# A decoder layer on one core: the moving operands of the split products stored with tokens reversed and read with step minus one

## The chip, the cores and the metric

The kernel runs on one core of one Trainium2 chip, in one launch. The metric is the device time of the launch in microseconds. Work on the host (laying out weights, transposing the input and the output) is not part of it.

## The reference, cut to what matters

One layer on 512 tokens of width 1024, all in float32. Three blocks are added to the residual stream in turn:

```python
x = x + 0.5 * swiglu(rms_norm(x, g_ffn1), w_ffn1_gate, w_ffn1_up, w_ffn1_down)
proj = rms_norm(x, g_mix) @ w_in          # q, k, v, u, mq
...                                       # window attention, conv module, memory attention
x = x + concatenate([y_attn, y_conv, y_mem], axis=-1) @ w_out
x = x + 0.5 * swiglu(rms_norm(x, g_ffn2), w_ffn2_gate, w_ffn2_up, w_ffn2_down)

def swiglu(x, w_gate, w_up, w_down):
    return (silu(x @ w_gate) * (x @ w_up)) @ w_down
```

The hidden width of each SwiGLU is 2816, 22 tiles of 128. The middle block projects to queries, keys, values, a gated convolution input and memory queries. It does attention in a window of 128 tokens with a sink per head, a causal convolution of 31 taps with a layer norm, and attention into 256 memory tokens, and projects the three results back. Almost all of the arithmetic is in the matrix products with weights.

## The kernel before, in words

**Layout.** Features lie on the 128 partitions and tokens along the free dimension: `x` is a tile of 128 x 8 x 512. A product of a weight tile with activations has the weights as the stationary operand (128 x 128, loaded into the array for each matmul) and the activations as the moving operand, 512 or 256 tokens at a time. The result lands in PSUM as 128 features x tokens.

**Split products.** To keep float32 accuracy at the speed of the rounded type `float32r`, each operand is stored as a sum of two rounded parts, hi and lo. A product is then three matmuls: hi x hi, hi x lo, lo x hi, added up in PSUM. `mm3` (L339 to L349) issues the three for a list of feature tiles; `product` (L439 to L446) does the same for the blocks described below. The hi part is written by ScalarE (a copy that rounds), the lo part by VectorE (the value less its hi part).

**Moving operands of these products.** All of them are hi and lo tiles of this kind:

- `xh`, `xl`: `x` times the norm's gain, written by `scaled_split` (L354 to L359), 8 tiles of each in each stage, read 512 tokens at a time;
- `hh`, `hl`: the hidden activations of a SwiGLU, written by `hidden` (L400 to L403), read 512 tokens at a time in the first of six rounds of the down projection and in two halves of 256 after it (`cut` in `mm3`);
- `yh`, `yl`: the outputs of the three parts of the middle block, written by `put_y` (L977 to L979);
- `bh`, `bl`: seven blocks of 256 tokens for each pair of feature tiles, written by `blocks` (L417 to L437);
- `mh`, `ml`: the memory tokens, 256 at a time, written by `piece` (L588 to L608). They are the moving operand of L347 to L349 in `part1`, and the stationary operand of L646 to L648, where weights move.

The tiles `xh`, `xl`, `hh`, `hl`, `mh`, `ml` and some of `yh`, `yl` come from one pool of 20 slots through `atile` (L291).

**Gate and up products.** The first 4 hidden tiles of a SwiGLU are plain (`ffn`, the `else` of L523: 48 matmuls of 512 columns each). The other 18 (`fast`, L448) use a scheme with seven block products in place of eight: gate and up weights and left and right halves of the features are combined in sums, which `make_sums` and `blocks` prepare, and each product has 12 matmuls of 256 columns.

**Weights.** `Weights` (L86) streams the weight tiles from memory on SyncE's queue, in the order in which they are used and three ahead, and splits each into hi and lo (L167 on ScalarE, L168 on VectorE). The four pairs of `whi` and `wlo` tiles are used in turn. Each is 1,056 elements wide for 1,024 that are used; the argument `off` of `add` says by how many bytes the hi part is moved up in it (0 or 128), the lo part lies at the other end of the spare room. Two small tiles named `shift` (L287 and L430) are not used by any instruction; they move what is allocated after them by 128 and 64 bytes.

**Order.** The program is written out instruction by instruction for each engine, with semaphores for what depends on what. The middle block follows a list written by hand (`ORDER`, L65). SyncE's queue loads weights and stores the output; ScalarE's and GpSimd's queues carry a few small transfers and sums.

Of the kernel before, what the change touches and what calls it, by code (L numbers as in the profile page):

```python
# [31 lines left out]
F32R = mybir.dt.float32r  # L32
# [6 lines left out]
P = 128  # L39
T = 512  # L40
KT = 8
# [37 lines left out]
N_ACT = 20  # L79
# [128 lines left out]
def layer(tc, ctx, a):  # L208
# [10 lines left out]
    def nm(s):  # L219
        uid[0] += 1  # L220
        return f"{s}_{uid[0]}"
# [10 lines left out]
    def work():  # L232
        return tmp.tile([P, T], F32, tag="t", name=nm("t"), bufs=5)
# [54 lines left out]
    act = ctx.enter_context(tc.tile_pool(name="act", bufs=1))  # L288
    xh, xl = {}, {}

    def atile(name, dtype=F32R):  # L291
        return act.tile([P, T], dtype, tag="h", name=nm(name), bufs=N_ACT)

    nc.scalar.dma_start(par, a["par"])
    warm = tmp.tile([P, T], BF16, tag="t", name="warm", bufs=5)
# [58 lines left out]
    def scaled_split(d, gcol):  # L354

        g = par[:, gcol + d : gcol + d + 1]
        xh[d], xl[d] = atile("xh"), atile("xl")
        ACT.activation(xh[d], x[:, d], AF.Identity, scale=g)
        DVE.scalar_tensor_tensor(xl[d], x[:, d], g, xh[d].bitcast(F32), op0=ALU.mult, op1=ALU.subtract)  # L359
# [34 lines left out]
    def ffn(pool, norm, first, gain, hooks, next_gain, last):  # L394
# [3 lines left out]
        bh, bl = {}, {}  # L398

        def hidden(f, t):  # L400
            h_hi[f], h_lo[f] = atile("hh"), atile("hl")
            ACT.copy(h_hi[f], t)
            DVE.tensor_tensor(h_lo[f], t, h_hi[f].bitcast(F32), op=ALU.subtract)  # L403
# [13 lines left out]
        def blocks(k):  # L417

            raw = pool.tile([P, 4, 256], F32, tag="sum", name=nm("braw"), bufs=SUM_BUFS)
            made = pool.tile([P, 4, 256], F32, tag="sum", name=nm("bmade"), bufs=SUM_BUFS)  # L420
            flat_raw = raw.rearrange("p a b -> p (a b)")
            for i, d in enumerate((k + 4, k)):
                DVE.scalar_tensor_tensor(
                    flat_raw[:, i * T : (i + 1) * T], x[:, d], par[:, gain + d : gain + d + 1], rb, op0=ALU.mult, op1=ALU.mult
                )
            b21, b22, b11, b12 = (raw[:, i] for i in range(4))
            bh[k] = pool.tile([P, 7, 256], F32R, tag="bh", name=nm("bh"), bufs=4)
            bl[k] = pool.tile([P, 7, 256], F32R, tag="bl", name=nm("bl"), bufs=4)
            if k == 0:
                pool.tile([P, 16], F32, name=nm("shift"))  # L430
            ACT.copy(bh[k][:, 4:7], raw[:, 0:3])
            DVE.tensor_tensor(made[:, B_T3 : B_Q1 + 1], raw[:, 1:3], raw[:, 3:4].to_broadcast([P, 2, 256]), op=ALU.subtract)
            DVE.scalar_tensor_tensor(made[:, B_Q2], made[:, B_T3], -1.0, b11, op0=ALU.mult, op1=ALU.subtract)
            DVE.tensor_tensor(made[:, B_T4], b21, made[:, B_Q2], op=ALU.add)
            ACT.copy(bh[k][:, 0:4], made)
            DVE.tensor_tensor(bl[k][:, 4:7], raw[:, 0:3], bh[k][:, 4:7].bitcast(F32), op=ALU.subtract)
            DVE.tensor_tensor(bl[k][:, 0:4], made, bh[k][:, 0:4].bitcast(F32), op=ALU.subtract)  # L437
# [80 lines left out]
        for f in range(NF):  # L518
# [4 lines left out]
            if f >= N_DIRECT:  # L523
                fast(f, mid)
            else:
                g, u = (sc_bank(), sc_bank()) if f % 3 == 2 else (mm_bank(), mm_bank())
                gh, gl = W.next()
                if f == 0:
                    uh, ul = W.next()
                    for ks in first:  # L530
                        mm3(g, gh, gl, ks, xhk, xlk, ks[0] == 0, ks[-1] == 7)
                        mm3(u, uh, ul, ks, xhk, xlk, ks[0] == 0, ks[-1] == 7)
                    norm.stats()
                    held = (g, u)
                else:
                    mm3(g, gh, gl, range(8), xhk, xlk, True, True)
                    if f == 1:
                        norm.spread()
                        raw[0] = evac(0, *held)
                        blocks(0)  # L540
                        hidden(0, raw[0])
                    uh, ul = W.next()
                    mm3(u, uh, ul, range(8), xhk, xlk, True, True)
                    raw[f] = evac(f, g, u)
                    if f == 1:
                        hidden(1, raw[1])
                    blocks(f)
                if f == N_DIRECT - 1:
                    for i in range(2, N_DIRECT):
                        hidden(i, raw[i])  # L550
# [29 lines left out]
    def memory():  # L580
# [7 lines left out]
        def piece(c):  # L588
                mh, ml = st.setdefault("mh", []), st.setdefault("ml", [])
                raw = st["raw", c]  # L590
                hi, lo = atile("mh"), atile("ml")
                sq = work()
                r0 = 0
                ACT.activation(sq, raw[:, r0 : r0 + T], AF.Square)
                for j in range(2):
                    k = 2 * c + j
                    g = par[:, C_GMEM + k : C_GMEM + k + 1]
                    r = raw[:, r0 + j * ML : r0 + (j + 1) * ML]
                    s = slice(j * ML, (j + 1) * ML)
                    ACT.activation(hi[:, s], r, AF.Identity, scale=g)  # L600
                    DVE.scalar_tensor_tensor(lo[:, s], r, g, hi[:, s].bitcast(F32), op0=ALU.mult, op1=ALU.subtract)
                mh.append(hi)
                ml.append(lo)
                if c == 0:
                    st["tot"] = tmp.tile([P, T], F32, tag="sqsum", name="mtot", bufs=1)
                    ACT.copy(st["tot"], sq)
                else:
                    POOL.dma_start(st["tot"], sq, accum_op=ALU.add)  # L608
# [65 lines left out]
        def part2():  # L674
# [5 lines left out]
            DVE.tensor_tensor(m, m, ps, op=ALU.mult)  # L680

        return load, piece, sums, part1, part2


# [55 lines left out]
    with tc.tile_pool(name="mix", bufs=1) as mix:  # L740
        norm = mixing(tc, nc, a, mix, W, norm, locals())
# [5 lines left out]
def mixing(tc, nc, a, mix, W, norm, e):  # L747
# [4 lines left out]
    mm3, xhk, xlk, rsqrt, nm = (e[n] for n in ("mm3", "xhk", "xlk", "rsqrt", "nm"))  # L752
    scaled_split, Norm = e["scaled_split"], e["Norm"]

    atile = e["atile"]
    spare = (N_ACT - 2 * KT) // 2
    yh = [atile("yh") if k < spare else mix.tile([P, T], F32R, name=f"yh{k}") for k in range(KT)]
    yl = [atile("yl") if k < spare else mix.tile([P, T], F32R, name=f"yl{k}") for k in range(KT)]
    pad = mix.tile([P, 2, T + 32], F32, name="pad")
    conv = mix.tile([P, 2, T], F32, name="conv")  # L760
    kT = mix.tile([P, T], F32, name="kT")
# [473 lines left out]
```

## Time and profile before

| | |
|---|---|
| time of the launch, median of 3 runs | 865.7 us (864.17 to 868.23) |
| span of the profiled execution | 862.3 us |
| TensorE busy | 855.5 us (99%), 6361 matmuls |
| weight loads of TensorE busy | 789.7 us (92%), 6361 loads |
| VectorE busy | 697.0 us (81%) |
| ScalarE busy | 446.1 us (52%) |
| GpSimd busy | 27.4 us (3%) |
| read from memory | 85.45 MB, 102 GB/s over the span |

The profile is of one execution. Its span runs from the first to the last instruction; the time of the launch contains a little more than that, and the profile gives no launch time of its own execution. Matmuls are pipelined: the next begins before the one before it has ended, so the durations of matmuls in the rows overlap, and what a matmul costs is read from the distance between two starts. `PE` is TensorE's matmul, `PEld` its weight load, `DVE` VectorE, `ACT` ScalarE, `POOL` GpSimd, `SP` SyncE. A row of a group names line, engine, operation, `output<-inputs`, shapes and count, then the busy time and the mean duration in ns, then the idle time before it and what ended it. A row of a timeline has the start, the duration and the instruction. A row of a window has its bounds and length, the busy time with the count of instructions that touch it, the granted clock, and the DMA share and rate.

### The profile page before, as it was taken

The page shows a single profiled execution, that of the slowest core. Times are in us where ns is not written, and L with a number is a line of the kernel's source. Part 1 is how long each engine was busy: PE and PEld are TensorE (multiplying, and loading weights), DVE is VectorE, ACT ScalarE, POOL GpSimd, SP SyncE. Part 2 cuts the span into 40 slices and gives each one's busy share as a digit, 9 for nine tenths or more (in the row PEclk, how much of TensorE's full clock was granted, in tenths as well). Part 3 has the DMA queues.
Part 4 walks back from the last instruction along what each step waited for, and adds up shares of the span by engine and source line. Part 5 has one row for each costly group of instructions (what it writes and reads, how often), then busy time and mean ns, then how long its engine had stood idle before and what let it go on. Part 6 is the DMA issues. An engine that isn't in the chain of part 4 may idle for free.

```text
span 862.3 us, 15722 instructions
## 1 busy us (share of the span) xinstructions
PE 855.5 (99%) x6361; PEld 789.7 (92%) x6361; DVE 697.0 (81%) x1163; ACT 446.1 (52%) x741; POOL 27.4 (3%) x30
## 2 busy tenths in 40 slices
PE   9999999999999999999999999999999999999998
PEld 5889999999999999988776888889999999999998
DVE  7998877877868897869989985997887868787772
ACT  7455555455654444533948763454654544544540
POOL 0000000000000000300000030010000000000000
PEclk9999999999999999999999999999999999999999
DMA  7326333334553334222010423335333343323312
GB/s 273 123 78 168 97 100 122 100 112 133 142 143 120 123 110 130 74 98 62 5 57 14 133 75 103 94 91 154 99 98 123 98 122 97 109 92 100 120 49 99
DMA packets 34809, 91.45 MB, mean 106 GB/s; under 512 B 3248, under 2 KB 5808, under 8 KB 34736
## 3 DMA queue, kind: packets, MB, share of 16 engines
q1 hardware_dynamic: 32000, 85.99, 32.1%
q0 software_dynamic: 1584, 2.88, 2.1%
q10 hardware_dynamic: 1152, 1.57, 0.6%
q8 instruction: 50, 0.82, 0.4%
q14 instruction: 23, 0.19, 0.1%
HBM read 85.45 MB, written 2.10 MB: 102 GB/s over the span
## 4 chain that ended last, share of the span: by engine, by line
PE 92%; DVE 3%; ACT 2%; issue 1%; DMA 1%; SPq 0%; ACTq 0%; DVEq 0%
PE mm L347 14%; PE mm L349 14%; PE mm L348 14%; PE mm L444 11%; PE mm L445 11%; PE mm L446 11%; PE sc L444 2%; PE sc L445 2%; PE sc L446 2%; PE sc L349 1%; PE sc L347 1%; PE sc L348 1%; PE tp L948 1%; PE tp L962 1%; ACT p L913 1%
## 5 line engine op out<-in xcount | busy, mean ns | idle before, releaser
L444 PE MATMUL mm<-bh,whi 128*128 128x256 f32 x864 | 238.8, 276 | 0.2 <-ACT kept L459 0.2
L445 PE MATMUL mm<-bl,whi 128*128 128x256 f32 x864 | 238.5, 276 | 0.0
L446 PE MATMUL mm<-bh,wlo 128*128 128x256 f32 x864 | 238.5, 276 | 0.0
L348 PE MATMUL mm<-hl,whi 128*128 128x256 f32 (+1 forms) x640 | 183.9, 288 | 0.0
L349 PE MATMUL mm<-hh,wlo 128*128 128x256 f32 (+1 forms) x640 | 183.9, 288 | 0.0
L347 PE MATMUL mm<-hh,whi 128*128 128x256 f32 (+1 forms) x640 | 183.3, 288 | 0.0
L167 ACT CAST whi<-wraw 128x1024 fp32r<-128x1024 f32 (+2 forms) x122 | 124.2, 1021 | 102.5 <-PE mm L348 37.9
L168 DVE TENSOR_TENSOR wlo<-wraw,whi 128x1024 fp32r<-128x1024 f32 (+2 forms) x122 | 144.5, 1187 | 27.9 <-ACT whi L167 27.3
L444 PEld LDWEIGHTS mm<-bh,whi 128*128 128x128 f32 x864 | 162.2, 188 | 0.6 <-ACT kept L459 0.4
L445 PEld LDWEIGHTS mm<-bl,whi 128*128 128x128 f32 x864 | 162.2, 188 | 0.2
L446 PEld LDWEIGHTS mm<-bh,wlo 128*128 128x128 f32 x864 | 162.2, 188 | 0.0
L349 PEld LDWEIGHTS mm<-hh,wlo 128*128 128x128 f32 x640 | 120.2, 188 | 2.9
L347 PEld LDWEIGHTS mm<-hh,whi 128*128 128x128 f32 x640 | 120.2, 188 | 2.7
L348 PEld LDWEIGHTS mm<-hl,whi 128*128 128x128 f32 x640 | 120.2, 188 | 2.7
L168 DVE TENSOR_TENSOR wlo<-s,whi 128x1024 fp32r<-128x1024 f32 x72 | 87.9, 1222 | 34.7 <-ACT whi L167 34.4
L167 ACT CAST whi<-s 128x1024 fp32r<-128x1024 f32 x72 | 75.5, 1051 | 46.1 <-PE mm L445 42.3
L347 PE MATMUL mm<-xh,whi 128*128 128x512 f32 x192 | 76.6, 403 | 0.3 <-ACT whi L179 0.3
L348 PE MATMUL mm<-xl,whi 128*128 128x512 f32 x192 | 75.6, 394 | 0.6 <-DVE xl L359 0.5
L349 PE MATMUL mm<-xh,wlo 128*128 128x512 f32 x192 | 75.9, 395 | 0.0
L506 DVE SCALAR_TENSOR_TENSOR x<-mm,x 128x512 f32<-128x512 f32 x80 | 54.0, 682 | 3.3 <-PE mm L349 3.3
L167 ACT CAST vhi<-wraw 128x512 fp32r<-128x512 f32 x36 | 22.4, 622 | 60.9 <-PE sc L445 46.8
L126 DVE TENSOR_TENSOR s<-wraw 128x512 f32<-128x512 f32 x36 | 24.9, 691 | 33.5 <-DMA wraw<-in_wgu 33.5
(244 smaller groups left out, 1368.2 us busy)
## 6 DMA issues: line engine op xcount, KB each, us to landing
wraw<-in_wgu SPq DMA_DIRECT2D x86, 512.0 KB, 3.6
wraw<-in_wd SPq DMA_DIRECT2D x44, 512.0 KB, 3.6
wraw<-in_win SPq DMA_DIRECT2D x12, 512.0 KB, 3.5
x<-t POOLq DMA_DIRECT2D x8, 256.0 KB, 6.1
out<-t SPq DMA_DIRECT2D x7, 256.0 KB, 2.0
x<-in_xT SPq DMA_DIRECT2D x3, 512.0 KB, 6.8
wraw<-in_wout_a SPq DMA_DIRECT2D x6, 256.0 KB, 2.9
wraw<-in_wgu SPq DMA_DIRECT2D x4, 256.0 KB, 5.4
```

Of the source, the lines that this page charges most:

```text
L126: nc.vector.tensor_tensor(s12[:, l], u[:, l], u[:, r], op=ALU.add)
L167: nc.scalar.copy(hi[:, :cols], raw[:, :cols])
L168: nc.vector.tensor_tensor(lo[:, :cols], raw[:, :cols], hi[:, :cols].bitcast(F32), op=ALU.subtract)
L347: PE.matmul(ps[:, t], wh[:, w], hi(k)[:, t], start=one, stop=False, skip_group_check=cut > 1)
L348: PE.matmul(ps[:, t], wh[:, w], lo(k)[:, t], start=False, stop=False, skip_group_check=cut > 1)
L349: PE.matmul(ps[:, t], wl[:, w], hi(k)[:, t], start=False, stop=end, skip_group_check=cut > 1)
L444: PE.matmul(ps, wh[:, c], bh[k][:, block], start=one, stop=False, skip_group_check=not first)
L445: PE.matmul(ps, wh[:, c], bl[k][:, block], start=False, stop=False, skip_group_check=not first)
L446: PE.matmul(ps, wl[:, c], bh[k][:, block], start=False, stop=end, skip_group_check=not first)
L506: DVE.scalar_tensor_tensor(o, ps, 0.5, xd, op0=ALU.mult, op1=ALU.add)
L913: ACT.activation(self.p[n, h][:, c], src[h][:, i, c], AF.Exp, scale=self.fac[:, m : m + 1], bias=self.neg[:, m : m + 1], accum_out=self.de ...
L948: PE.transpose(ps[:, i * P : (i + 1) * P], self.p[n, h][:, c : c + P], ident)
```

## The change

The tiles of the moving operands are handed out as views with the token axis turned round (`[::-1]`). Writers and readers use the same view, so the value of token 0 is stored in the last place, and a matmul that reads tokens in rising order reads memory in falling order, with step minus one. For `bh` and `bl` the order inside each block of 256 is turned; the blocks stay in their places. `mh` and `ml` are turned a second time, which gives the plain order. The results in PSUM, the weights and all other tiles are as before.

```diff
     def atile(name, dtype=F32R):
-        return act.tile([P, T], dtype, tag="h", name=nm(name), bufs=N_ACT)
+        return act.tile([P, T], dtype, tag="h", name=nm(name), bufs=N_ACT)[:, ::-1]
...
-            bh[k] = pool.tile([P, 7, 256], F32R, tag="bh", name=nm("bh"), bufs=4)
-            bl[k] = pool.tile([P, 7, 256], F32R, tag="bl", name=nm("bl"), bufs=4)
+            bh[k] = pool.tile([P, 7, 256], F32R, tag="bh", name=nm("bh"), bufs=4)[:, :, ::-1]
+            bl[k] = pool.tile([P, 7, 256], F32R, tag="bl", name=nm("bl"), bufs=4)[:, :, ::-1]
...
-                hi, lo = atile("mh"), atile("ml")
+                hi, lo = atile("mh")[:, ::-1], atile("ml")[:, ::-1]
...
-    yh = [atile("yh") if k < spare else mix.tile([P, T], F32R, name=f"yh{k}") for k in range(KT)]
-    yl = [atile("yl") if k < spare else mix.tile([P, T], F32R, name=f"yl{k}") for k in range(KT)]
+    yh = [atile("yh") if k < spare else mix.tile([P, T], F32R, name=f"yh{k}")[:, ::-1] for k in range(KT)]
+    yl = [atile("yl") if k < spare else mix.tile([P, T], F32R, name=f"yl{k}")[:, ::-1] for k in range(KT)]
```

## The prediction

> **What bounds the kernel now.** I read the page first: the engines, the granted clock, and the chain of work that ended last.
>
> ```profile
> span 862.3 us, 15722 instructions
> ...
> PE 855.5 (99%) x6361; PEld 789.7 (92%) x6361; DVE 697.0 (81%) x1163; ACT 446.1 (52%) x741; POOL 27.4 (3%) x30
> ...
> PEclk9999999999999999999999999999999999999999
> ...
> PE 92%; DVE 3%; ACT 2%; issue 1%; DMA 1%; SPq 0%; ACTq 0%; DVEq 0%
> ```
>
> TensorE is never idle, its clock is full in every slice, and 92% of the chain is its own matmuls. So what counts is how soon one matmul follows another. The change touches the moving operand of nearly all of them. Their number comes from the groups by line with shapes kept apart; of each group I show the first of its three lines, since L347 to L349 and L444 to L446 issue three matmuls each time and the counts are equal.
>
> ```profile
> L444 PE MATMUL mm<-bh,whi 128*128 128x256 f32 x864 | 238.8, 276 | 0.2 <-ACT kept L459 0.2
> L444 PE MATMUL sc<-bh,vhi 128*128 128x256 f32 x144 | 39.8, 276 | 0.0
> L347 PE MATMUL mm<-hh,whi 128*128 128x256 f32 x576 | 159.0, 276 | 0.0
> L347 PE MATMUL mm<-hh,whi 128*128 128x512 f32 x64 | 24.3, 395 | 0.0
> L347 PE MATMUL mm<-xh,whi 128*128 128x512 f32 x192 | 76.6, 403 | 0.3 <-ACT whi L179 0.3
> L347 PE MATMUL sc<-xh,whi 128*128 128x512 f32 x32 | 12.6, 394 | 0.0
> L347 PE MATMUL mm<-yh,whi 128*128 128x512 f32 x48 | 18.6, 405 | 1.1 <-DVE s L895 1.0
> L347 PE MATMUL sc<-yh,whi 128*128 128x512 f32 x16 | 6.1, 394 | 0.0
> ```
>
> Of 256 columns there are 3 x (864 + 144 + 576) = 4,752, of 512 columns 3 x (64 + 192 + 32 + 48 + 16) = 1,056. The durations in these rows overlap, so the price of a matmul is the distance between starts. I take it from the count of a stretch (busy time by window) and the first and last start in it (timeline). First 256 columns, then 512 columns from xh and xl, then 512 columns from hh and hl:
>
> ```profile
> 650.00:700.00 50.00, 50.00 (x444) 1.00 0.35 104
> ...
> 649.73 0.28 PE L348 MATMUL mm<-hl,whi 128*128 128x256 f32 x1
> ...
> 699.94 0.28 PE L347 MATMUL mm<-hh,whi 128*128 128x256 f32 x1
> ...
> 545.00:560.00 15.00, 15.00 (x67) 1.00 0.24 71
> ...
> 544.71 0.39 PE L347 MATMUL mm<-xh,whi 128*128 128x512 f32 x1
> ...
> 559.81 0.39 PE L347 MATMUL mm<-xh,whi 128*128 128x512 f32 x1
> ...
> 580.40:584.00 3.60, 3.60 (x17) 1.00 1.05 279
> ...
> 580.21 0.40 PE L348 MATMUL mm<-hl,whi 128*128 128x512 f32 x1
> ...
> 583.94 0.40 PE L349 MATMUL mm<-hh,wlo 128*128 128x512 f32 x1
> ```
>
> 256 columns: (699.94 - 649.73) / 443 = 113.3 ns. 512 columns: (559.81 - 544.71) / 66 = 228.8 ns from xh and xl, and (583.94 - 580.21) / 16 = 233.1 ns from hh and hl. Together the matmuls whose operand is turned take 4,752 x 113.3 + 864 x 228.8 + 192 x 233.1 ns = 538 + 198 + 45 = 781 us of the 862.3 us span. One nanosecond on each is 5.8 us.
>
> Two more readings say what these distances hang on. The first is a row of weight loads with almost no matmul between them (two moving columns each), the second the one group of 256-column matmuls that runs slower.
>
> ```profile
> 393.92 0.86 PEld L826 LDWEIGHTS tp<-pair,t 128*128 128x128 f32 x7
> ...
> L826 PEld LDWEIGHTS tp<-pair,t 128*128 128x128 f32 x56 | 7.0, 191 | 1.5 <-issue 1.1
> ...
> L348 PEld LDWEIGHTS mm<-xl,whi 128*128 128x128 f32 x192 | 36.2, 189 | 9.1 <-DVE xl L359 1.9
> ...
> L349 PE MATMUL mm<-mh,wlo 128*128 128x256 f32 x16 | 4.5, 281 | 0.0
> ...
> 265.20 0.28 PE L348 MATMUL mm<-ml,whi 128*128 128x256 f32 x1
> ...
> 270.73 0.29 PE L646 MATMUL mm<-whi,mh 128*128 128x256 f32 x1
> ```
>
> Seven loads of 128 columns start in 0.86 us less the last one's own 0.191 us (mean of all its 56 loads, next row): 0.67 / 6 = 111.7 ns from one to the next. No kernel that loads weights for every matmul gets below that, so the 256-column matmuls stand 1.6 ns above their floor. The mh group (3 x 16 matmuls, L347 to L349 in part1) takes (270.73 - 265.20) / 47 = 117.7 ns each, 4.4 ns more, with the same shape and clock. And hh against xh above: 4.3 ns for the same shape and clock. What differs there is where the weights lie: those of hh are stored 128 bytes further along (`W.add(..., 128)`) than those of xh. So where, or when, the two reads of the array run against each other does matter, by a few nanoseconds.
>
> **The change, part by part.** Tiles, their addresses, the matmuls, their order, waits and DMAs stay. The view turns storage round; each matmul reads the same 1 or 2 KB from its other end. The mh and ml tiles are turned twice, which is plain order, so their 117.7 ns and L646 to L648 cost nothing new.
>
> The writers (ACT L358, L402, L431, L435, L978; DVE L359, L403, L436, L437, L979) now store backwards, and DVE reads one operand backwards too. No row shows a negative step. The nearest are a DVE instruction that reads rows of 256 with a repeated row and one that reads plainly:
>
> ```profile
> L475 DVE TENSOR_TENSOR t<-kept,mm 128x512 f32<-128x512 f32 x36 | 24.5, 681 | 5.9 <-PE mm L446 4.7 <-ACT kept L473 0.7
> L464 DVE TENSOR_TENSOR t<-mm,kept 128x512 f32<-128x512 f32 x36 | 24.6, 685 | 0.0
> L403 DVE TENSOR_TENSOR hl<-t,hh 128x512 fp32r<-128x512 f32 x36 | 24.6, 684 | 0.0
> L359 DVE SCALAR_TENSOR_TENSOR xl<-x,par,xh 128x512 fp32r<-128x512 f32 x24 | 24.8, 1035 | 8.2 <-ACT xh L358 8.0
> ```
>
> 681 against 685 ns: the pattern costs nothing, and I take 0. Cover is TensorE's own work; what is not covered are the turns between stages, where L359 stands in the chain. If a backward write took twice as long, that would cost at most L359's 24.8 us; below nothing I see no reason.
>
> The matmuls are the term that decides. No row shows a moving operand read backwards. A gain is bounded by the weight loads: 1.6 ns x 4,752 = 7.6 us, and for 512 columns, taken as two of 256 at that floor (223.4 ns), 5.4 x 864 + 9.7 x 192 ns = 6.5 us. A loss has as its nearest bound the slower spacings that the trace has: 117.7 for 113.3 ns, and 233.1 for 228.8 ns. Further out, the widest 256-column matmul after a pause is 10 ns longer than usual:
>
> ```profile
> L646 PE MATMUL mm<-whi,mh x16: 276/276/286, 270.7 to 275.9; 128*128 128x256 f32 x16
> ```
>
> I take the nearest slower spacing. Turning the read changes the relation between the two walks through memory at every start: the moving read begins 1,020 or 2,044 bytes from where it began, the weights stay. Such a relation is worth 4 ns in the trace either way, and 538 of the 781 us stand within 1.6 ns of the floor, so a new relation can hardly be better there and has room to be worse. 4,752 x 4.4 = 20.9 us, 864 x 4.3 = 3.7 us, the hh group of 512 columns unchanged: +24.6 us. The span becomes 886.9 us. The median of the runs, 865.7 us, lies 3.4 us over the profiled span of 862.3 us; that is added again: **890 us**.
>
> **The rivals.**
>
> *Direction is of no account (866 us).* If the array's two reads never meet, a pattern of another sign costs what the old one did: +0. For it: same bytes, same count, and the weight loads alone nearly explain 113.3 ns. Against it: 233.1 against 228.8 ns, and 117.7 against 113.3 ns. [...]
>
> *The walks get out of each other's way (852 us): the other side.* If turning the moving read makes it meet the weight read less often, both widths fall to their floors: -7.6 - 6.5 = -14.1 us. For it: there is 5 to 10 ns over the floor in every 512-column matmul, though the weight load beside it (189 ns for L348) is shorter than it. Against it: the 256 columns have little left to give. It decides once the 256-column spacing rises by less than 6.5 us / 4,752 = 1.4 ns: from there the 512 columns carry the sign. [...]
>
> *The backward read is a slow one (1,190 us).* If the moving read has to give way during each weight load for half of it, each matmul gains 55.9 ns: 5,808 x 55.9 = 325 us. For it: nothing in the trace, but nothing excludes it either, as every moving read in it runs upwards. It would show as some 296 matmuls of 256 columns where 50 us hold 444 now.
>
> **How the numbers follow.** Slower by the spacings that the trace has: 0.35. Walks out of each other's way: 0.34. Direction of no account: 0.16. Slow backward read: 0.15. The first has its own range from half its sum (878) to the 10 ns of the widest row, 4,752 x 10 = 47.5 us and 3.7 us on top of 865.7 (917). The range reaches down to the other side's 852 and 0.5% under it, 848, and up to 917; beyond lie the slow read and a little at the bottom. A measurement tells from no change what is over 0.5%, some 4 us. Faster: 0.33, nearly all of the other side. Same: 0.17. Slower: 0.35 + 0.15 = 0.50.
>
> **What would show it.** Same instruction counts, addresses, DMA bytes. In 650 to 700 us the 444 matmuls become about 427 if 117.7 ns holds, 450 at the floor, and stay 444 if direction is of no account; the L444 group's mean goes from 276 to about 281 ns or stays. The mh group stays at 281 ns. L403 and L359 stay at 684 and 1,035 ns. I am wrong if the 256-column spacing stays under 114.7 ns, and wrong in mechanism if the time moves while these spacings stand.

## The result, and the profile after

The changed kernel takes 888.6 us (median of 4 runs, 888.5 to 889.0) against 865.4 us (864.2 to 868.2) for the kernel before on the same chip: a ratio of 1.027, with a 95% interval of 1.024 to 1.029. It is slower. The profiled execution spans 886.3 us, 24.0 us more than before.

The page of the kernel after, its head, engines, clock and chain:

```profile
span 886.3 us, 15722 instructions
...
PE 880.2 (99%) x6361; PEld 812.1 (92%) x6361; DVE 701.8 (79%) x1163; ACT 447.9 (51%) x741; POOL 27.4 (3%) x30
...
PEclk9999999999999999999999999999999999999999
...
PE 96%; ACT 1%; DVE 1%; DMA 1%; issue 0%; SPq 0%; DVEq 0%
```

As many instructions as before, the same full clock (1.000 in both executions), and TensorE still busy for 99% of the span. The whole difference has to be in the distance between matmuls. The groups by line of the kernel after, shapes kept apart (busy us, mean ns of one, then the idle time before them):

```profile
L444 PE MATMUL mm<-bh,whi 128*128 128x256 f32 x864 | 243.7, 282 | 0.0
L347 PE MATMUL mm<-hh,whi 128*128 128x256 f32 x576 | 162.4, 282 | 0.0
L347 PE MATMUL mm<-xh,whi 128*128 128x512 f32 x192 | 77.1, 406 | 0.0
L359 DVE SCALAR_TENSOR_TENSOR xl<-x,par,xh 128x512 fp32r<-128x512 f32 x24 | 24.8, 1035 | 8.3 <-ACT xh L358 8.1
L403 DVE TENSOR_TENSOR hl<-t,hh 128x512 fp32r<-128x512 f32 x36 | 24.6, 685 | 0.0
L347 PE MATMUL mm<-hh,whi 128*128 128x512 f32 x64 | 24.4, 396 | 0.0
...
L646 PE MATMUL mm<-whi,mh 128*128 128x256 f32 x16 | 4.5, 281 | 0.0
L349 PE MATMUL mm<-mh,wlo 128*128 128x256 f32 x16 | 4.4, 276 | 0.0
```

The turned matmuls of 256 columns went from 276 to 282 ns in the lines shown (279 and 280 ns where `bl` and `hl` are read). The writers did not move: 1,035 and 685 ns, where 1,035 and 684 stood. And the two groups with plain operands, which were to stay as they were, have changed places: the mh group fell from 281 to 276 ns, and L646 rose from a median of 276 (277 in the mean) to 281.

Now the distances themselves, in the same way as before: busy time by window with the count of matmuls that touch it, and the first and last start of that stretch.

```profile
650.00:700.00 50.00, 50.00 (x427) 1.00 0.33 105
...
649.77 0.28 PE L446 MATMUL mm<-bh,wlo 128*128 128x256 f32 x1
...
699.95 0.28 PE L446 MATMUL sc<-bh,vlo 128*128 128x256 f32 x1
```

256 columns: (699.95 - 649.77) / 426 = 117.8 ns, where 113.3 stood. For the other groups I set the window's bounds on the start of a first and a last matmul, so that the length is that of a known number of distances:

```profile
272.41:277.74 5.33, 5.33 (x48) 1.00 0.69 193
277.74:283.28 5.54, 5.54 (x50) 1.00 0.58 199
...
557.99:566.39 8.40, 8.40 (x38) 1.00 0.00 0
590.42:597.42 7.00, 7.00 (x32) 1.00 0.99 208
```

The mh group has 47 distances in 5.33 us: 113.4 ns. L646 to L648 have 47 in 5.54 us: 117.9 ns. Thirty-six matmuls from xh and xl take 8.40 us: 233.3 ns, where 228.8 stood. Thirty from hh and hl take 7.00 us: 233.3 ns, where 233.1 stood.

Over all starts of the two traces the mean of the turned 256-column matmuls goes from 113.37 to 118.05 ns and that of the 512-column ones from x and y from 229.4 to 233.5 ns; distances over 160 ns at 256 columns and over 300 ns at 512 are left out as pauses. That is 4,752 x 4.68 = 22.2 us and 864 x 4.0 = 3.5 us, 25.7 us together. The pauses behind these matmuls sum to 19.9 us where they were 21.6, so 1.6 us came back. That leaves 24.1 us, and the span grew by 24.0.

### The profile page after: what moved, and what is told of

Same layout as the page of the kernel before. It is cut to its first block, busy times and chain, and to the rows that moved or that the text cites. A ratio compares the mean times of both kernels' runs of the same rounds, so it can differ in the third digit from the quotient of the medians.

```text
span 886.3 us, 15722 instructions
## 1 busy us (share of the span) xinstructions
PE 880.2 (99%) x6361; PEld 812.1 (92%) x6361; DVE 701.8 (79%) x1163; ACT 447.9 (51%) x741; POOL 27.4 (3%) x30
## 4 chain that ended last, share of the span: by engine, by line
PE 96%; ACT 1%; DVE 1%; DMA 1%; issue 0%; SPq 0%; DVEq 0%
PE mm L347 16%; PE mm L349 15%; PE mm L348 15%; PE mm L444 12%; PE mm L446 12%; PE mm L445 11%; PE sc L444 2%; PE sc L446 2%; PE sc L445 2%; PE sc L349 1%; PE sc L348 1%; PE sc L347 1%; PE tp L948 1%; PE tp L962 1%; ACT p L913 1%; DMA x<-in_xT 1%
## 5 line engine op out<-in xcount | busy, mean ns | idle before, releaser
L444 PE MATMUL mm<-bh,whi 128*128 128x256 f32 x864 | 243.7, 282 | 0.0
L446 PE MATMUL mm<-bh,wlo 128*128 128x256 f32 x864 | 243.6, 282 | 0.0
L445 PE MATMUL mm<-bl,whi 128*128 128x256 f32 x864 | 241.3, 279 | 0.0
L349 PE MATMUL mm<-hh,wlo 128*128 128x256 f32 (+1 forms) x640 | 187.3, 293 | 0.0
L347 PE MATMUL mm<-hh,whi 128*128 128x256 f32 (+1 forms) x640 | 186.7, 293 | 0.0
L348 PE MATMUL mm<-hl,whi 128*128 128x256 f32 (+1 forms) x640 | 185.9, 291 | 0.0
L168 DVE TENSOR_TENSOR wlo<-wraw,whi 128x1024 fp32r<-128x1024 f32 (+2 forms) x122 | 145.2, 1190 | 42.2 <-ACT whi L167 41.4
L349 PEld LDWEIGHTS mm<-hh,wlo 128*128 128x128 f32 x640 | 120.1, 188 | 2.9
L465 ACT ACTIVATE t<-t 128x512 f32<-128x512 f32 x36 | 22.7, 631 | 52.2 <-DVE t L464 52.2
```

The lines of the kernel that those rows point to most:

```text
L168: nc.vector.tensor_tensor(lo[:, :cols], raw[:, :cols], hi[:, :cols].bitcast(F32), op=ALU.subtract)
L347: PE.matmul(ps[:, t], wh[:, w], hi(k)[:, t], start=one, stop=False, skip_group_check=cut > 1)
L348: PE.matmul(ps[:, t], wh[:, w], lo(k)[:, t], start=False, stop=False, skip_group_check=cut > 1)
L349: PE.matmul(ps[:, t], wl[:, w], hi(k)[:, t], start=False, stop=end, skip_group_check=cut > 1)
L444: PE.matmul(ps, wh[:, c], bh[k][:, block], start=one, stop=False, skip_group_check=not first)
L445: PE.matmul(ps, wh[:, c], bl[k][:, block], start=False, stop=False, skip_group_check=not first)
```

## The experiments

To tell the placements apart I give each a **distance**: the address where the moving read starts, less the address where the next matmul's weight read starts (in the compiled program that read goes through the columns from the last one down), in bytes modulo 256. Both addresses are read off the compiled program; no trace holds them. In the kernel before it is 196 for all matmuls of 256 columns and for the 512-column ones from hh, and 68 for those from xh and yh. In the kernel after, 192, 192 and 64. The mh group and L646 to L648, with their plain operands, are at 196 in both kernels. Five theories are named in the expectations. R: only this relation of the two reads counts. D: the direction counts. S: at one placement there are two steady rhythms of 256-column matmuls, 113.3 and 117.7 ns, and the way in decides. W: the weight read beside a matmul holds its moving read up, for as long as it lasts. N: a read with step minus one is slower by itself.

### The turned kernel at three other placements, the plain one at one

The two unused `shift` tiles are given other sizes, which moves the moving operands against the weights; nothing else changes. The edit of the turned and of the plain kernel with 64 bytes more is the same:

```diff
-    tmp.tile([P, 32], F32, name="shift")
+    tmp.tile([P, 48], F32, name="shift")
...
-                pool.tile([P, 16], F32, name=nm("shift"))
+                pass
```

The other two turned kernels have 64 and 48 elements in these places, and 80 and 32.

Expected of the turned kernel with 64 bytes more:

> Turned operands as in the changed kernel, but stored 64 bytes further along against all weights. Theory R (placement: only where the moving read starts against the weight read counts, the direction does not): the 256-column spacing leaves 117.7 ns, and some placement of the turned operand gives back 113.3 ns; with 4,752 matmuls at 113.3 ns the time is some 867 us. Theory D (direction: a moving read that runs the same way as the weight read costs 4.4 ns wherever it starts): 117.7 ns stays, some 888 us. Theory S (two steady rhythms, 113.3 and 117.7 ns, exist for both directions, and the start of a stretch decides which one is fallen into): exactly one of these two numbers per stretch, perhaps both in one run.

with 128 bytes more:

> Turned operands stored 128 bytes further along against all weights, which exchanges the placements of the 256-column and the 512-column matmuls. R: the 256-column spacing leaves 117.7 ns, and the 512-column matmuls of xh stand apart from those of hh again (they are at 233.3 and 233.2 ns in the changed kernel). D: 117.7 ns and 233 ns stay, some 888 us. S: 113.3 or 117.7 ns.

with 192 bytes more:

> Turned operands stored 192 bytes further along. R: of the four placements 0, 64, 128, 192 at least one gives 113.3 ns for 256 columns. D: 117.7 ns in all four, some 888 us. S: 113.3 or 117.7 ns.

of the plain kernel with 64 bytes more:

> The kernel before, operands in plain order, stored 64 bytes further along against all weights. R: the 256-column spacing rises from 113.3 ns to 117 ns or more, since the start of the read is as far from where it was in the kernel before as any; some 885 us. D: the direction is the plain one, 113.3 ns stays, 865 us. S: 113.3 or 117.7 ns.

Measured, one run each; the kernel before took 864.5 us on that chip. Spacings are means over all starts of the trace, pauses left out as above (for the kernel before, of the trace that the prediction shows):

| kernel | time, us | 256 columns: distance, ns | 512 from x: distance, ns | 512 from hh: distance, ns |
|---|---|---|---|---|
| before | 864.5 | 196, 113.4 | 68, 229.4 | 196, 233.2 |
| after | 888.6 | 192, 118.1 | 64, 233.4 | 192, 233.3 |
| turned, +64 | 891.3 | 0, 118.3 | 128, 233.9 | 0, 233.3 |
| turned, +128 | 899.1 | 64, 120.0 | 192, 233.4 | 64, 233.4 |
| turned, +192 | 899.0 | 128, 120.0 | 0, 233.5 | 128, 233.3 |
| plain, +64 | 897.1 | 4, 120.0 | 132, 233.0 | 4, 227.6 |

The window 650 to 700 us, first of the turned kernel with 128 bytes more, then of the plain one with 64:

```profile
650.00:700.00 50.00, 50.00 (x419) 1.00 0.36 107
```

```profile
650.00:700.00 50.00, 50.00 (x419) 1.00 0.36 111
```

Both hold 419 matmuls, 120.0 ns each. So a plain kernel can be as slow as the slowest turned one: placement is worth 6.6 ns of a plain matmul, and R has that right. But none of the four turned placements came below 117.8 ns or 233.3 ns, which speaks for D. Four placements cannot tell whether the fast one was just not among them.

### Only the blocks turned

```diff
-            bh[k] = pool.tile([P, 7, 256], F32R, tag="bh", name=nm("bh"), bufs=4)
-            bl[k] = pool.tile([P, 7, 256], F32R, tag="bl", name=nm("bl"), bufs=4)
+            bh[k] = pool.tile([P, 7, 256], F32R, tag="bh", name=nm("bh"), bufs=4)[:, :, ::-1]
+            bl[k] = pool.tile([P, 7, 256], F32R, tag="bl", name=nm("bl"), bufs=4)[:, :, ::-1]
```

> Only the blocks bh and bl are turned (3,024 of the 4,752 matmuls of 256 columns); xh, xl, hh, hl, yh, yl stay plain. If the cost is paid matmul by matmul, L444 to L446 take 118 ns and L347 to L349 113.3 ns, and the time rises by 3,024 x 4.6 ns = 14 us, to some 879 us. If the rhythm of one group carries over into the next (theory S), the hh matmuls of 256 columns that follow the blocks at once take 118 ns too, and the time is some 887 us.

Measured: 878.5 us (878.0 to 879.9), ratio 1.012 (1.007 to 1.017). Its groups by line, and the window 650 to 700 us:

```profile
L444 PE MATMUL mm<-bh,whi 128*128 128x256 f32 x864 | 243.3, 282 | 0.0
L347 PE MATMUL mm<-hh,whi 128*128 128x256 f32 x576 | 159.9, 278 | 0.0
...
650.00:700.00 50.00, 50.00 (x433) 1.00 0.36 106
```

The blocks pay 117.8 ns each (3,024 x 4.4 = 13.3 us), the plain matmuls of 256 columns from hh and hl 114.3 in the mean. That is the size of the difference of the medians, 13.1 us: the price is paid matmul by matmul by those that are turned. (The trace is of the longest of the four executions, in which the hh group's 0.9 ns add 1,728 x 0.9 = 1.6 us.) But the hh group, whose addresses, order and direction are those of before, isn't quite at 113.4. Behind a turned stretch its first three distances are mostly 115 to 120 ns before it comes back to 113 and 114. And at 345.4 us, where one distance is 148 ns, it goes over to 117.8 ns and stays there for its last 180 distances; in the kernel before the same 180, behind a distance of 154 ns, ran at 113.3.

### Appended stretches: 12 placements in either direction

To measure the matmuls by themselves I appended stretches of equal matmuls to the kernel before; their results go nowhere. `d` is the offset of the moving operand in elements, `cols` the width of the weights:

```python
def stretch(turned, d, n, cols, count):
    ps = mm_bank()
    mv = bm[:, d : d + n]
    if turned:
        mv = mv[:, ::-1]
    for i in range(count):
        PE.matmul(ps[:cols, :n], bw[:, (i % 8) * P : (i % 8) * P + cols], mv, start=i == 0, stop=i == count - 1)
```

> The kernel before, followed by 65 stretches of matmuls that only measure: one moving tile, plain or turned, at 12 placements from 0 to 224 bytes in steps down to 4 bytes, 256 or 512 columns, against weights of 128 or of 64 columns; their results are not used. The time of the launch is longer by about the stretches and says nothing; the spacings count. Theory W (the moving read is held up by the weight read beside it): with weights of 64 columns what a matmul takes over its bare columns shrinks to about half, for 512 columns from 233 ns to some 223 ns, in both directions. Theory N (a read with step minus one is slower by itself): turned 512-column matmuls stay at 233 ns with weights of 64 columns too. Placement: if finer steps than 64 bytes help the turned read, some turned placement of 256 columns shows 113.3 ns; theory D (direction) has all turned placements at 117.7 ns or more. The plain read is at 113.3 ns at the placement of the kernel before (192 bytes) and at 120 ns 64 bytes on.

Windows of this kernel whose bounds are the first and the last start of a stretch of 40 matmuls of 256 columns: plain at distance 4, plain at 196, turned at 192. Then of 24 matmuls of 512 columns: plain at 68, turned at 64.

```profile
865.02:869.70 4.68, 4.68 (x41) 1.00 0.00 0
912.30:916.73 4.43, 4.43 (x42) 1.00 0.00 0
969.22:973.82 4.60, 4.60 (x41) 1.00 0.00 0
1012.15:1017.41 5.26, 5.26 (x24) 1.00 0.00 0
1079.40:1084.77 5.37, 5.37 (x25) 1.00 0.00 0
```

The stretches repeat what the kernels do: 4.68 / 39 = 120.0 ns, 113.6 (113.3 once settled), 117.9; 5.26 / 23 = 228.7 and 233.5 ns. From here on spacings are means over the second half of a stretch. Plain matmuls of 256 columns ran at 113.3 ns at two of the twelve placements (20 and 196) and at 116.7 to 123.4 at the others. Turned ones ran at 117.8 to 120.0 at all twelve. Plain ones of 512 columns ran at 226.7 to 236.7 ns, turned ones at 233.3 at ten placements and slower at two. With weights of 64 columns, at four placements, the turned ones stayed at 117.8 to 120.1 and 233.3 ns; the plain ones ran at 113.4 to 119.0 ns (113.4 at distance 4, 119.0 at 196) and 228.3 to 232.6. The 223 ns at 512 columns that W expected came in neither direction; that figure was my estimate, and it takes off a time for the bare columns that no run shows.

### All 64 placements

Every distance in steps of 4 bytes, in both directions; 36 matmuls of 256 columns in the first kernel:

```diff
+        stretch(False, 0, 256, 128, 36)
+        stretch(False, 1, 256, 128, 36)
...
+        stretch(True, 63, 256, 128, 36)
```

and 20 of 512 columns in the second:

```diff
+        stretch(False, 0, 512, 128, 20)
...
+        stretch(True, 63, 512, 128, 20)
```

> The kernel before, followed by stretches of 36 matmuls of 256 columns that only measure, results not used: plain and turned reading at all 64 placements of the moving tile in steps of 4 bytes, weights of 128 columns. Theory D (direction: a turned read has no good placement): all 64 turned placements lie at 117 ns or above, while a few plain ones show 113.3 ns. Theory R (placement alone): turned placements with 113.3 ns exist, about as many as plain ones; a turned kernel with the tiles put there would be at 865 us.

> The same with stretches of 20 matmuls of 512 columns. D: the turned read lies at 233.3 ns at nearly every placement and nowhere below, the plain one between 226 and 238 ns. R: the turned read reaches 226 to 229 ns at some placement too.

Windows of the first kernel, from the first to the last of 36 starts: plain at distance 20 and at 108, turned at 20 and at 32:

```profile
876.72:880.68 3.96, 3.96 (x37) 1.00 0.00 0
970.95:975.49 4.54, 4.54 (x37) 1.00 0.00 0
1155.69:1159.88 4.19, 4.19 (x37) 1.00 0.00 0
1168.76:1172.89 4.13, 4.13 (x38) 1.00 0.00 0
```

| | lowest, ns | mean of 64, ns | highest, ns | where |
|---|---|---|---|---|
| 256, plain | 113.3 | 119.2 | 130.0 | 113.3 at 4 of 64: distances 20, 116, 148, 196 |
| 256, turned | 117.8 | 120.1 | 123.7 | 117.8 at 32, 96, 160, 224; 120.0 at 52 of 64 |
| 512, plain | 226.7 | 233.1 | 240.3 | 226.7 at 0, 4, 32, 64, 112, 160 |
| 512, turned | 233.3 | 235.6 | 241.9 | 233.3 at 27 of 64 |

This goes further than the four kernels could: in none of the 64 placements did a turned stretch reach what the plain read has at its best. It also suggests why the kernel before loses so much. In the mean over placements, turning costs 0.9 ns at 256 columns and 2.4 ns at 512. The kernel before stands on one of the four placements whose plain stretch ran at 113.3 ns, so it has 4.4 ns to lose.

One stretch for each placement is one sample, though. The turned read at distance 192 stands at 120.0 ns in the map, at 117.9 in the earlier run of twelve placements and at 118.1 in the kernel after. The plain mh matmuls of the turned kernel with 128 bytes more, at distance 68, ran at 113.3 ns, where the map has 117.8.

### Weights of 32 columns, and the way into the rhythm

The next kernel has stretches with weights of 32 columns at four placements, and twelve stretches at the placements of the two kernels, each behind the same eight products of one column:

```diff
+        stretch(False, 0, 256, 32, 40)
+        stretch(False, 16, 256, 32, 40)
...
+        stretch(True, 0, 256, 32, 40)
...
+        small_ones()
+        stretch(False, 48, 256, 128, 40)
+        small_ones()
+        stretch(False, 48, 256, 128, 40)
...
+        small_ones()
+        stretch(True, 48, 256, 128, 40)
...
```

> The kernel before, followed by stretches that only measure, results not used. First, 512 and 256 columns, plain and turned, at 4 placements, against weights of only 32 columns: if the weight read beside it holds the moving read up for as long as it lasts (W), a quarter of the load leaves some 219 ns of the 233.3 ns; if the load's length is of no account, 233.3 ns stays for the turned read. Then the placement of the kernel before (196 bytes from weight to moving start, plain, 256 columns) eight times, each time right after 8 matmuls of one column. If two rhythms exist at one placement (S), some of these stretches settle at 117.7 ns and not at 113.3 ns, as the mh matmuls of the kernel before did; if placement fixes the spacing, all eight show the same. Then the turned read four times in the same way: 117.7 to 120 ns, never 113.3 ns.

Windows of this kernel from first to last of 40 starts: weights of 32 columns plain and turned; then weights of 128 columns, plain at distance 196, the first and the second of its eight stretches; then turned at 192:

```profile
903.66:908.09 4.43, 4.43 (x40) 1.00 0.01 4
921.84:926.43 4.59, 4.59 (x42) 1.00 0.02 4
942.40:947.08 4.68, 4.68 (x42) 1.00 0.00 0
948.90:953.42 4.52, 4.52 (x41) 1.00 0.02 4
993.32:998.00 4.68, 4.68 (x41) 1.00 0.01 4
```

In the last three windows the first distance is some 200 ns, behind the one-column products, and is not part of the rhythm: (4.68 - 0.20) / 38 = 117.9 ns in the first of them.

Two readings. With 32 columns the plain matmuls run at 113.3 ns at all four placements (the one at distance 4 as well, which stood at 120.0 with 128 columns), while the turned ones stay at 117.7 to 118.3 and 233.3 ns. So what placement does to the plain read depends on the width of the weights, and what direction does is something else. W itself has only part of this right: the 219 ns that it expected, an estimate with the same time for the bare columns, did not come, since the plain matmuls of 512 columns ran at 231.3 to 231.7 ns. And of the eight equal plain stretches with weights of 128 columns, seven settled at 113.3 ns within six matmuls, and the first stayed at 117.75 to its end: the same instructions at the same addresses have two rhythms, as S says. What decides between them is not shown; ahead of its one-column products the first stretch has a turned stretch, the seven others a plain one. All four turned ones stood at 117.7 to 117.9.

### The 512-column weights stored for a faster placement

Could the plain kernel gain from the map? I stored the weights of the 512-column matmuls (all but 48 of those from hh and hl) 36 bytes up in their tiles, hi and lo alike, to distances 32 and 160, where plain stretches had run at 226.7 ns:

```diff
-                    for t, c in (("whi", off // 4), ("wlo", 32 - off // 4))
+                    for t, c in (("whi", off // 4), ("wlo", 32 - off // 4 if off % 128 == 0 else off // 4))
...
-                W.add(down(*d), 128)
+                W.add(down(*d), 36)
...
-        W.add(flat(a["win"][t]))
+        W.add(flat(a["win"][t]), 36)
...
```

> The kernel before, plain reading, with the weights of all 512-column products (gate and up of the first 4 tiles, w_in, w_out, the first round of the down projections) stored 36 bytes up in their tiles, hi and lo alike, so that their matmuls have the placements 32 and 160 bytes, which the stretches showed at 226.7 ns. If the placement found there holds in the kernel, 512-column matmuls go from 228.8 and 233.2 ns to about 227 ns: 864 x 2 ns + 192 x 6 ns = some 2.9 us less, 862.5 us. If the mixed order of the kernel has other rhythms than the stretches, the gain is smaller or turns into a loss of up to 864 x 4.5 ns = 4 us.

Measured: 876.7 us (870.9 to 881.8, 6 runs) against 865.7 us (864.1 to 871.6, 11 runs), ratio 1.010 (1.007 to 1.014): about 1% longer, where 2.9 us less or at most 4 us more had been expected. In the profiled execution (881.8 us, the longest of the six) the 512-column matmuls stand at 231.4 to 232.6 ns, not at 226.7; in the kernel hi and lo tiles take turns, in the stretch one tile is read again and again. Whether that is why was not shown. But the greater loss is in matmuls that the edit didn't touch. The group, the window, and two more windows of this kernel with the two matmuls between them; then the same place in the kernel before:

```profile
L444 PE MATMUL mm<-bh,whi 128*128 128x256 f32 x864 | 242.1, 280 | 0.3 <-ACT kept L459 0.3
...
650.00:700.00 50.00, 50.00 (x427) 1.00 0.34 106
...
100.00:119.00 19.00, 19.00 (x170) 1.00 0.30 88
121.00:140.00 19.00, 19.00 (x163) 1.00 0.44 133
...
119.47 0.28 PE L446 MATMUL mm<-bh,wlo 128*128 128x256 f32 x1
120.02 0.39 PE L444 MATMUL mm<-bh,whi 128*128 128x256 f32 x1 [0.27 <-ACT kept L459]
```

```profile
100.00:119.00 19.00, 19.00 (x171) 1.00 0.31 90
121.00:140.00 19.00, 19.00 (x170) 1.00 0.39 131
...
119.45 0.28 PE L446 MATMUL mm<-bh,wlo 128*128 128x256 f32 x1
119.90 0.38 PE L444 MATMUL mm<-bh,whi 128*128 128x256 f32 x1 [0.18 <-ACT kept L459]
```

The blocks, plain and at distance 196 as before, take 280 ns and stand 427 to the window, as in the kernel after. They were in the slow rhythm of S for most of the time, and the trace shows where they fell into it. Up to 119.5 us they run at 113.3 ns. TensorE then waits once for ScalarE (L459), and the next 1,270 distances settle at 117.8 ns. From 283 us on they stand at 113.3 again, and from 591 us, behind matmuls of 512 columns, at 117.8 to the end. The kernel before has the same pause at the same place, 450 ns from start to start against 550 here, and goes on at 113.3 ns. In the mean the 256-column matmuls cost 3.4 ns more, 4,752 x 3.4 = 16 us of the 17.3 us by which this execution's span (879.6 us) is longer. So the kernel before holds its 113.3 ns not by placement alone. Whether the edit brings the slow rhythm about by shifting the pauses, or each execution falls one way or the other, stays open: only this one of the six has a trace. No version here beats the kernel before.

### Weights of 2 columns

What is the turned read's price when there is next to no weight read beside it?

```diff
+        stretch(False, 0, 512, 2, 24)
...
+        stretch(True, 0, 512, 2, 24)
...
+        stretch(False, 0, 256, 2, 40)
...
+        stretch(False, 0, 128, 2, 40)
...
```

> The kernel before, with 56 measuring stretches appended whose results are used by nothing: 24 matmuls of 512 columns or 40 of 256, plain or turned, at four placements of the moving operand, with weights of 2, 8 and 16 columns in place of 128, and eight stretches of 128 columns. With 32 columns the plain matmuls of 256 columns stood at 113.3 ns at all four placements, and the turned ones at 117.7 to 118.3 and 233.3 ns as with 128 columns. If a turned read only loses by meeting the read of the weights (theory W), then with 2 columns there is next to nothing left to meet, and turned and plain come to the same spacing within 1 ns. If the read with step minus one has a price of its own (theory N), the turned ones stay at 117.7 and 233.3 ns with 2 columns too, and the plain ones stand at 113.3 and 226.7 ns or below at every placement. If the price comes with the start of a read and not with its length, the turned 128 columns lose the same 4 to 7 ns; if it goes by the column, 2 to 3 ns. The kernel itself takes the 860 us of before ahead of them.

Windows of this kernel from first to last start, weights of 2 columns, plain and then turned each time: 24 matmuls of 512 columns, 40 of 256, 40 of 128:

```profile
860.72:866.03 5.31, 5.31 (x25) 1.00 0.14 49
882.95:888.32 5.37, 5.37 (x25) 1.00 0.01 3
905.35:909.79 4.44, 4.44 (x40) 1.00 0.00 0
923.57:928.16 4.59, 4.59 (x41) 1.00 0.01 4
1105.91:1108.24 2.33, 2.33 (x41) 1.00 0.00 0
1110.70:1113.04 2.34, 2.34 (x42) 1.00 0.03 7
```

256 columns: 113.35 ns plain and 117.75 to 117.8 turned, at each of four placements. 512 columns: 231.1 to 231.7 plain, 233.3 turned. 128 columns: 60.0 both ways. With 8 and 16 columns the turned ones stood at 117.7 to 117.9 ns (one stretch at 120.0) and 233.3, the plain ones at 113.3 (one stretch of the eight at 116.7) and 228.8 to 231.7. W falls as the reason of the change's cost, and N stands: the turned read pays 4.4 ns at 256 columns with almost nothing read beside it. What N expected of its size did not come out in either form. The price is neither one per start (nothing at 128 columns) nor one by the column (2 ns at 512). And the plain 512-column matmuls did not fall to 226.7 ns: they ran at 231.7 ns with weights of 2 columns, slower than the 228.8 to 229.4 that those from x have in the kernel before with 128.

Weights that are walked upwards, so that both reads turn their direction together, were not tried: in the compiled programs they are always read from the last column down.

## Why the prediction was right, and where it was not

**The bound.** "What counts is how soon one matmul follows another" held: same instructions, same clock, 427 matmuls in the window where about 427 had been named for 117.7 ns.

**The terms of the sum.** The turned 256-column matmuls were to gain 4.4 ns and 20.9 us; they gained 4.7 ns and 22.2 us. In the kernel after they do not sit at the even 117.7 of the mh group, but in a pattern of 120, 115 and 118 ns, with some stretches a little slower. The 512-column ones from x and y were to gain 4.3 ns and 3.7 us; they gained 4.0 ns and 3.5 us. The hh group of 512 columns was to stay, and did (233.1 and 233.3). The sum left out that slower matmuls shorten the waits for others: 1.6 us came back. So the span grew by 24.0 us for a forecast of 24.6. The rest of the miss (890.3 us before rounding, against 888.6) is in the allowance for what lies around the span: 3.4 us in the prediction, 888.6 - 886.3 = 2.3 us with the profile after.

**The writers.** Backwards stores and reads on VectorE and ScalarE cost nothing: on VectorE 684 became 685 ns and 1,035 stayed 1,035, on ScalarE (L402) 622 stayed 622.

**The step that failed** is "The mh and ml tiles are turned twice, which is plain order, so their 117.7 ns and L646 to L648 cost nothing new", and with it the sign "The mh group stays at 281 ns". It fell to 276 ns, and L646 to L648 rose to 281. Together that is no time (47 distances 4.3 ns shorter, 47 4.1 ns longer), but it breaks the reasoning: what I took for the mark of a placement was one of two rhythms that the same placement can have. Both groups are at distance 196 in both kernels. The eight equal stretches show the two rhythms by themselves, and the kernel with moved weights, which goes from one to the other at a pause, shows them at the scale of a kernel.

**The reason given for the loss** was "the relation between the two walks through memory at every start". The nearest slower spacing was the right number for another reason: 117.7 ns was the slow rhythm of a plain group, not a new relation of two walks. Whether the turned read's own 117.8 is that same rhythm, which it never leaves, the runs do not show. So it is in part luck that 890 us came so near to 888.6. The relation does matter, and by more than I said (113.3 to 130.0 ns over the 64 placements). But the 4.4 ns are there with weights of 2 columns at every placement tried, so they belong to the turned read itself. At 512 columns two parts can be told apart: 1.7 to 2.3 ns are the turned read's own with weights of 2 columns. The rest would be the good meeting with the weights at distance 68, where the plain read stands 1.7 to 2.8 ns below its 231.1 to 231.7 with weights of 2 columns; the turned read had no such gain in any stretch. Why a turned read is slower, and why at 256 and 512 columns but not at 128, stays open.

**The bound of the gain** was taken from the weight loads, 111.7 ns apart. Weights of 2 columns left the plain matmuls at 113.3 ns, so it is not the width of the loads that holds them there. Nor are 111.7 ns the floor of such loads: in the trace before, the transposes of L948, each with its load of 128 columns, start 109 ns apart (median). The runs show nothing to gain by turning, and the rival at 852 us, to which I gave 0.34, had less to stand on than its row seemed to say: no turned stretch came below 117.6 or 233.3 ns, and in the five kernels with turned operands no 18 distances in a row between turned 256-column matmuls had a mean below 117.6.

**The other rivals.** "Direction is of no account" (866 us) is off by some 23 us. Its condition, that the array's two reads never meet, does not agree with these runs: the same plain matmul takes 113.3 to 130.0 ns by where its operand lies against the weights. The slow backward read (1,190 us) was right in that a backward read has a price of its own. But its mechanism, giving way to the weight load, fell with W, and its price was twelve times too high: 4.7 ns, not 55.9.

## What to carry to other kernels

Where matmuls follow each other without a pause, read their cost from counts and starts in a window, and look for groups of one shape that stand at different distances (117.7 and 113.3 ns in the kernel before): such a pair says what a change of layout can cost, though not by itself why. Keep moving operands of 256 and 512 columns in rising order (no turned stretch came below 117.6 and 233.3 ns, where plain ones reached 113.3 and 226.7), and treat any shift of addresses, even of another operand, as a change to be measured (876.7 against 865.7 us with weights moved by 36 bytes). Compare the spacing before and behind a pause as well: equal matmuls can come out of it in another rhythm, as those of the kernel with moved weights did, 113.3 ns ahead of a pause and 117.8 behind it. A kernel that stands at the best spacing seen has everything to lose by moving: the plain kernel moved by 64 bytes took 897.1 us for 864.5.

## What the runs showed of the hardware that was not expected

- The plain 256-column matmul has its best spacing, 113.3 ns, at 4 of 64 placements with weights of 128 columns (one stretch each), and at all four placements tried with weights of 2, 16 or 32. The worst placement costs 130.0 ns.
- The same stretch of matmuls at the same addresses can settle at 113.3 or at 117.75 ns and stay there (seven of eight and one of eight). In a kernel, one pause of 550 ns from start to start was followed by 1,270 matmuls in the slow one.
- A narrower weight load does not always help: plain 512-column matmuls took 226.7 ns at the best placements with weights of 128 columns, and 231.1 to 231.7 with weights of 2.
- Many settled spacings lie on a grid: 60.0, 113.33, 120.0, 226.67 and 233.33 ns are 9, 17, 18, 34 and 35 times 6.667 ns, and the others seen often, 116.67 and 117.78, are 17 1/2 and 17 2/3 times that. What sets the step is open.
- The kernel before, unchanged, took 864.1 to 871.6 us over 11 runs on one chip. Whether its slower runs are those that fell into the other rhythm is open, since none of them has a trace.
